# Norm factors by transposes, and a fixed order for the end of a two-layer transformer kernel

## The chip, the cores and the metric

The kernel runs on one core of a Trainium2 chip. The metric is device time in microseconds (us), the median over runs. TensorE (PE in the views; PEld is its weight load), VectorE (DVE), ScalarE (ACT) and GpSimd (POOL) each work through a list of instructions of their own and wait for one another by semaphores; SyncE (SP), ACT and POOL issue the transfers (DMA) between memory and the on-chip buffers. Products land in PSUM, which the kernel uses as eight banks of 128 x 512 fp32.

## What is computed

Two layers of a latent-diffusion backbone over 512 latent tokens and 256 context tokens, D = 1024, all in float32. Each layer is an attention mixer and a SwiGLU feed-forward, both behind a modulated RMS norm, and the result is the RMS-normed latent stream:

```python
def rms_norm(x, gain=None):
    y = x * lax.rsqrt(jnp.mean(x * x, axis=-1, keepdims=True) + EPS)
    return y if gain is None else y * gain
...
for l in range(DEPTH):                      # 2 layers, the second without context output
    a = modulate(h, shift, scale)           # rms_norm(h) * (1 + scale) + shift
    h = h + g_a * mixer(a)                  # layer 0: latent + neighbourhood heads; layer 1: sliding window
    h = h + g_f * swiglu(modulate(h, ...), w_gate_up, w_down)
return rms_norm(h_lat, final_norm)
```

Layer 0 also norms the two low-rank projections of its latent attention (256 and 128 features, with a gain).

## The kernel before, in words

Activations are stored transposed: eight tiles (`KT`), each 128 features by 768 tokens (`LATS`, 512 columns; `CTXS`, 256). Every large product is made of three: weights and activations are split into a high part and a rest (`h`, `lo`), and `mm3` (L328) and `product` (L1367) multiply high by high, high by rest and rest by high into one bank.

**A norm** needs one factor per token, and tokens lie along the free dimension. So every norm goes the same way. ACT squares the eight tiles (`square_sum`, L369) and POOL or DVE adds them up. PE multiplies each block of 128 tokens of the sum, as weights, by a column of ones, which leaves that block's sums in one column of PSUM, tokens along the partitions (L388, L802, L980). ACT takes the root (L390), DVE the reciprocal (L391): a narrow tile `col`, 128 x (2 to 4) values. To bring the factors back along the free dimension, in every partition, DVE builds a block-diagonal matrix, identity times `col` (L392, L806, L988), and PE multiplies it from the left by a 128 x 128 matrix of ones (L397, L812, L992). In `rstd` the factors are then read where they are, in the one bank with the tag `o`; in `norm_spread` and `gained` ACT copies them to a buffer `r` first (L814, L993).

There are twelve such norms. `first_norm` and `norm_spread` (L799 to L814) make the two at the start, latents and context, with a hand-written order on PE (`run`). `gained` (L963) makes two in the neighbourhood attention, with the gains of the low-rank projections, as side work between the steps of the attention. `rstd` (L379) makes eight: two each for the ends of the four `output` stages (both mixers' and both feed-forwards' last products). The stage `output` (L1242) runs two streams, each eight products of one output tile with the residual added by DVE (`add_residual`, L1223), and the squares behind it; the norm of the first stream is threaded between the second stream's products.

**The end of the kernel** is such a stage (`final1`, L1622): the last four of the 22 feed-forward columns, so 12 products of 128 x 256 for each output tile and half of the tokens (`HALVES`); eight tiles for the first half, then eight for the second with the weights kept. POOL adds the first six squares of a half to the running sum and DVE the last. `finished` (L1610) multiplies a tile by its norm's factors and its gain and sends it out, even tiles by SP, odd ones by ACT.

**The order.** A planner places the instructions at build time, by their priority (the order in which the program emits them, moved by hand for side work) and by its own simulated times, and gives out buffers and banks as they come free (`SCHED`). `behind(x, y)` and `in_turn` pin one instruction behind another without a wait on the data. Much around the `rstd` norms is pinned so: where a norm falls among later products, its sums and its spreading stand ahead of set products of those (L1262, L1458). Banks have tags: three `s`, two `t`, two `d`, one `o`; products take them in turn (`PG`), the side work only `d` (`PQ`), and in the neighbourhood attention so does every third set of transposes of the attention weights (`turned`, L497). Those, and `spread` (L365), which brings the softmax sums back, are PE transposes already.

## Time and profile before

| | |
|---|---|
| median of 3 runs | 1594.34 us (1590.8 to 1597.15) |
| the profiled execution | 1595.19 us, its span 1593.4 us, so 1.8 us lie around the span |
| PE | busy 96% of the span |
| DVE, ACT, POOL | 74%, 50%, 19% |
| mean granted clock of PE | 0.988 |
| last record of the last product | starts at 1580.33 us of the span |

Times in the views are us from the start of the span. In a row of the timeline the first number is the start, the second the duration; rows of like instructions that follow each other are merged (x4), and the brackets give the idle time of the engine before and what ended it. One fp32 product shows as two records. A PE record is longer than its turn: the next one starts while it still drains, so the cost on PE is read from start to start. The name behind an operation is out<-in, and for a product the moving operand comes first, then the weights.

### The profile page before, as it was taken

What the parts mean: (1) busy time and instruction counts of PE and PEld (TensorE: products, weight loads), DVE (VectorE), ACT (ScalarE), POOL (GpSimd) and SP (SyncE); (2) the same over time, 40 slices, a digit from 0 to 9 for tenths busy, and PEclk for the clock granted to TensorE, in tenths of its full rate; (3) what the DMA queues carried; (4) which work ended last, traced back from release to release, by engine and by line L of the source; (5) the groups of instructions that cost most, each with busy time, mean ns of one, the idle gap of its engine ahead of it and who ended that gap; (6) DMA issues with size and microseconds to landing.
All of it is one profiled execution on the core that took longest, in us unless ns stands there. A gap on an engine that the chain in (4) does not pass through costs nothing. (4 is left out here: it accounts for less than half of the span.)

```text
span 1593.4 us, 26482 instructions
## 1 busy us (share of the span) xinstructions
PE 1533.9 (96%) x9966; PEld 1371.9 (86%) x9966; DVE 1177.1 (74%) x2348; ACT 797.9 (50%) x1615; POOL 299.3 (19%) x322
## 2 busy tenths in 40 slices
PE   6999999999999999999999998999999999999997
PEld 4787767787899999999989896877889899899997
DVE  4885877576678587796858686878877778678685
ACT  4563676775455243342424243557755545354453
POOL 0144623320011101102021202493012000000002
PEclk9999999999999999999999998999999999999998
DMA  9745332104343555637464756121015133324222
GB/s 309 252 129 178 84 117 59 23 6 159 129 162 127 190 168 167 215 114 289 152 248 158 268 165 248 61 87 60 2 46 168 47 100 126 107 79 133 87 93 80
DMA packets 76544, 214.91 MB, mean 135 GB/s; under 512 B 9952, under 2 KB 17504, under 8 KB 76416
## 3 DMA queue, kind: packets, MB, share of 16 engines
q1 hardware_dynamic: 57568, 141.79, 27.0%
q0 software_dynamic: 15968, 67.24, 12.2%
q10 hardware_dynamic: 2880, 4.20, 0.7%
q8 instruction: 78, 1.28, 0.3%
q14 instruction: 50, 0.41, 0.1%
HBM read 186.97 MB, written 23.07 MB: 132 GB/s over the span
## 5 line engine op out<-in xcount | busy, mean ns | idle before, releaser
L324 ACT CAST wh<-wr 128x1024 fp32r<-128x1024 f32 (+2 forms) x148 | 114.7, 789 | 199.8 <-DMA wr<-in_w_dn_dram 35.4
L325 DVE TENSOR_TENSOR wl<-wr,wh 128x1024 fp32r<-128x1024 f32 (+2 forms) x145 | 134.0, 930 | 81.6 <-ACT wh L324 79.9
L555 ACT ACTIVATE p<-p,sm 128x512 f32<-128x512 f32 (+3 forms) x144 | 105.0, 730 | 30.2 <-DVE sm L559 28.3
L376 POOL TENSOR_TENSOR p<-p,p 128x256 f32<-128x256 f32 (+1 forms) x33 | 32.2, 976 | 465.0 <-PE psd L338 340.5
L1372 PE MATMUL pss<-b,wh 128*128 128x384 f32 (+1 forms) x344 | 107.0, 311 | 0.6 <-ACT b L361 0.6
L1373 PE MATMUL pss<-b,wh 128*128 128x384 f32 (+1 forms) x344 | 107.2, 312 | 0.1
L1374 PE MATMUL pss<-b,wl 128*128 128x384 f32 (+1 forms) x344 | 106.2, 312 | 0.4 <-DVE wl L1360 0.4
L233 DVE CUSTOM_DVE_ANT_0 p<-rope,cond 128x1024 bf16<-128x1024 f32 x64 | 77.2, 1222 | 38.3 <-DMA rope<-in_mod_w_dram 38.3
L337 PE MATMUL psd<-b,wh 128*128 128x512 f32 (+3 forms) x256 | 87.9, 344 | 0.0
L335 PE MATMUL psd<-b,wh 128*128 128x512 f32 (+3 forms) x216 | 78.5, 364 | 0.5 <-ACT wh L324 0.3
L549 PE MATMUL pso<-ph,b 128*64 128x256 f32 (+1 forms) x384 | 77.5, 360 | 0.4 <-DVE ph L494 0.2
L549 PE MATMUL pso<-pl,b 128*64 128x256 f32 (+1 forms) x384 | 76.7, 359 | 0.7 <-DVE pl L494 0.7
L338 PE MATMUL psd<-b,wl 128*128 128x512 f32 (+3 forms) x216 | 76.6, 355 | 0.1
L228 POOL DMA_DIRECT2D rope<-in_mod_w_dram x48 | 25.5, 531 | 239.7 <-DVE mod L233 227.0
L1374 PE MATMUL pst<-b,wl 128*128 128x384 f32 (+1 forms) x224 | 70.1, 313 | 0.0
L1373 PE MATMUL pst<-b,wh 128*128 128x384 f32 (+1 forms) x224 | 69.9, 312 | 0.0
L1372 PE MATMUL pst<-b,wh 128*128 128x384 f32 (+1 forms) x224 | 69.9, 312 | 0.0
L335 PE MATMUL pss<-st,wh 128*128 128x512 f32 (+2 forms) x200 | 68.2, 342 | 1.6 <-ACT st L1173 0.8
L338 PE MATMUL pss<-st,wl 128*128 128x512 f32 (+2 forms) x200 | 68.0, 341 | 0.0
L337 PE MATMUL pss<-b,wh 128*128 128x256 f32 (+3 forms) x211 | 67.9, 322 | 0.1
L749 PE MATMUL pss<-st,st 128*128 128x256 f32 (+3 forms) x194 | 60.3, 333 | 6.2 <-DVE sm L559 5.9
L1372 PEld LDWEIGHTS pss<-b,wh 128*128 128x128 f32 x344 | 65.2, 190 | 1.1 <-ACT b L361 0.9
(666 smaller groups left out, 5412.9 us busy)
## 6 DMA issues: line engine op xcount, KB each, us to landing
wr<-in_w_gu_dram SPq DMA_DIRECT2D x88, 512.0 KB, 4.1
rope<-in_mod_w_dram POOLq DMA_DIRECT2D x48, 512.0 KB, 3.8
wr<-in_w_out_dram SPq DMA_DIRECT2D x32, 512.0 KB, 3.5
wr<-in_w_dn_dram SPq DMA_DIRECT2D x64, 256.0 KB, 3.0
p<-home POOLq DMA_DIRECT2D x40, 384.0 KB, 5.4
home<-p POOLq DMA_DIRECT2D x40, 384.0 KB, 4.9
wr<-in_w_in_dram SPq DMA_DIRECT2D x21, 512.0 KB, 4.1
nb<-in_nb_dram SPq DMA_DIRECT2D x16, 384.0 KB, 3.1
```

What stands on the lines that cost most here:

```text
L233: V.tensor_tensor_reduce(out=T("p", [P, D], mybir.dt.bfloat16), in0=w, in1=cond[:, v, :], op0=ALU.mult, op1=ALU.add, scale=1.0, scalar=0.0 ...
L324: behind(S.copy(h, r), *after[:1])
L325: behind((G if eng else V).tensor_tensor(lo, r, f(h), op=ALU.subtract), *after[1:])
L335: ins = PE.matmul(o, wh[:, k], mh[:, c], start=first and k == 0, stop=False)
L337: PE.matmul(o, wh[:, k], ml[:, c], start=False, stop=False)
L338: PE.matmul(o, wl[:, k], mh[:, c], start=False, stop=last and k == n - 1)
L549: ins = PE.matmul(o[64 * i : 64 * i + 64, c], v(kt), t, start=n == 0, stop=n == len(moving[i]) - 1)
L555: S.activation(p[:, c], p[:, c], AF.Exp, bias=nm, scale=-1.0, accum_out=dn)
L749: PE.matmul(o, x, ks[0][:, keys], start=True, stop=False)
L1372: PE.matmul(o, wh, xh, start=first and k == 0, stop=False, skip_group_check=not first)
L1373: PE.matmul(o, wh, xl, start=False, stop=False, skip_group_check=not first)
L1374: PE.matmul(o, wl, xh, start=False, stop=k == 3, skip_group_check=not first)
```

## The change

Three things are done.

1. **Factors by transposes.** No diagonal matrix is built. For each block of 128 tokens, `spread` transposes the column of `col`, read as 128 equal columns (`to_broadcast`), which writes the factors of the block along the free dimension of all 128 partitions. This replaces L392 and L397 in `rstd`, L806 and L812 at the start, and L988 and L992 in `gained`. The mark `diag`, behind which a residual of the second stream is pinned, is now the reciprocal.
2. **No copy in `gained`.** The new `gain` lets DVE multiply the tiles by the factors where they are, in the bank of tag `d`, in two pieces (512 and 256 columns), where ACT copied them to `r` and DVE multiplied 768 columns at once.
3. **A fixed order at the end.** `final1` no longer uses `output` and `Norm`. The table of the root is loaded by a dummy root behind the last SiLU. The squares are kept as four partial sums per half (tiles 0 to 3 added by POOL, 4 and 5 by DVE, 6 and 7 alone), and PE adds them up: eight products of one column into one bank, in a chain, of which the first alone clears the bank (`start`). In the second half the products of tiles 0 to 7 are pinned in order, the sums of the first half in front of tile 2, its spreading in front of tile 3, and DVE's order is pinned throughout: two outputs of the first half in front of each of the residuals 5, 6 and 7, and two after. The first half's outputs all go out by SP, the second's by SP and ACT in turn.

```diff
@@ -381,20 +381,19 @@
 
         n, accs = c.stop - c.start, [x for x in acc if x is not None] if type(acc) is list else [acc]
         m, d = n // P, get()
-        col, diag = T("sm", [P, 6, 2]), B(tag=tag)
-        col = col.rearrange("p a b -> p (a b)")[:, :m]
+        col = T("sm", [P, 6, 2]).rearrange("p a b -> p (a b)")[:, :m]
         for i in range(m):
             for j, a in enumerate(accs):
                 marks["sum"] = PE.matmul(d[:, i : i + 1], a[:, i * P : (i + 1) * P], ones[:, :1], start=j == 0,
                                          stop=j == len(accs) - 1)
         marks["root"] = S.activation(col, d[:, :m], AF.Sqrt, bias=eps, scale=1.0 / nfeat)
-        V.reciprocal(col, col)
-        marks["diag"] = V.tensor_tensor(diag[:, :n].rearrange("p (a b) -> p a b", b=P), ident.unsqueeze(1).to_broadcast([P, m, P]),
-                                        col.unsqueeze(2).to_broadcast([P, m, P]), op=ALU.mult)
+        marks["diag"] = V.reciprocal(col, col)
         for i in range(0, n, 512):
             w = min(512, n - i)
             d = get() if r is not None else PS("o")
-            marks["spread"] = PE.matmul(d[:, :w], ones, diag[:, i : i + w], start=True, stop=True)
+            for j in range(0, w, P):
+                at = (i + j) // P
+                marks["spread"] = spread(d[:, j : j + P], col[:, at : at + 1].to_broadcast([P, P]))
             if r is None:
                 return d
             S.copy(r[:, c.start + i : c.start + i + w], d[:, :w])
@@ -798,19 +797,17 @@
 
     def first_norm(acc, c):
         n, d = (c.stop - c.start) // P, PM()
-        col, diag = T("sm", [P, 6, 2]).rearrange("p a b -> p (a b)")[:, :n], B(tag="p")
+        col = T("sm", [P, 6, 2]).rearrange("p a b -> p (a b)")[:, :n]
         ins = [PE.matmul(d[:, i : i + 1], acc[:, i * P : (i + 1) * P], ones[:, :1], start=True, stop=True) for i in range(n)]
         run(ins[0], ins[-1])
         root = S.activation(col, d[:, :n], AF.Sqrt, bias=eps, scale=1.0 / D)
         V.reciprocal(col, col)
-        V.tensor_tensor(diag[:, : n * P].rearrange("p (a b) -> p a b", b=P), ident.unsqueeze(1).to_broadcast([P, n, P]),
-                        col.unsqueeze(2).to_broadcast([P, n, P]), op=ALU.mult)
-        return root, diag
-
-    def norm_spread(diag, c):
+        return root, col
+
+    def norm_spread(col, c):
         d = PM()[:, : c.stop - c.start]
-        ins = PE.matmul(d, ones, diag[:, : c.stop - c.start], start=True, stop=True)
-        run(ins, ins)
+        ins = [spread(d[:, i * P : (i + 1) * P], col[:, i : i + 1].to_broadcast([P, P])) for i in range((c.stop - c.start) // P)]
+        run(ins[0], ins[-1])
         S.copy(r[:, c], d)
 
     fetched = []
@@ -960,6 +957,17 @@
 
         return use
 
+    def gain(tiles, g0, col):
+
+        for c in (LATS, CTXS):
+            d, n = PQ(), c.stop - c.start
+            for i in range(n // P):
+                at = c.start // P + i
+                spread(d[:, i * P : (i + 1) * P], col[:, at : at + 1].to_broadcast([P, P]))
+            for j, t in enumerate(tiles):
+                V.scalar_tensor_tensor(t[:, c], t[:, c], gains[:, g0 + j : g0 + j + 1], d[:, :n], op0=ALU.mult, op1=ALU.mult)
+        return tiles
+
     def gained(groups):
 
         d, m = PQ(), NT // P
@@ -984,17 +992,7 @@
         V.reciprocal(col, col)
         yield
         for i, (tiles, g0) in enumerate(groups):
-            diag, r = B(), B()
-            V.tensor_tensor(diag.rearrange("p (a b) -> p a b", b=P), ident.unsqueeze(1).to_broadcast([P, m, P]),
-                            col[:, i * m : i * m + m].unsqueeze(2).to_broadcast([P, m, P]), op=ALU.mult)
-            for c in (LATS, CTXS):
-                d = PQ()
-                PE.matmul(d[:, : c.stop - c.start], ones, diag[:, c], start=True, stop=True)
-                S.copy(r[:, c], d[:, : c.stop - c.start])
-            res = []
-            for j, t in enumerate(tiles):
-                V.scalar_tensor_tensor(t, t, gains[:, g0 + j : g0 + j + 1], r, op0=ALU.mult, op1=ALU.mult)
-                res.append(split(t, V))
+            res = [split(t, V) for t in gain(tiles, g0, col[:, i * m : i * m + m])]
             groups[i] = res
             yield
 
@@ -1424,7 +1422,7 @@
 
         def tail(self):
             product(self.z, self.s4, self.ops["22"])
-            S.activation(self.s[:, self.c2], self.z, AF.Silu)
+            marks["silu"] = S.activation(self.s[:, self.c2], self.z, AF.Silu)
             product(self.y, self.u2, self.ops["T4"])
             V.tensor_tensor(self.t[:, self.c1], self.y, self.t[:, self.c1], op=ALU.add)
             for c in (self.c2, self.c1) if self.w > NX else (slice(0, 2 * self.w),):
@@ -1607,11 +1605,6 @@
     output(lambda m: I["w_out1"][m], O, 1, 2, ((HALVES[1], 0), (HALVES[0], 0)), norm, (0, 0), wait=1)
 
 
-    def finished(m, r, c, v):
-        o = B(tag="p")
-        V.scalar_tensor_tensor(o[:, c], H[m][:, c], fn[:, m : m + 1], r[:, c], op0=ALU.mult, op1=ALU.mult)
-        (nc.sync, nc.scalar)[m % 2 if OUTQ else 0].dma_start(out[m, :, c], o[:, c])
-
     fn = const("final_norm", [P, 8])
 
     def down1(m, w, hs):
@@ -1620,8 +1613,68 @@
         add_residual(m, o, 1, 5, 0, LATS)
 
     def final1(src, hs):
-        keep = lambda src, m: ahead.get(m) or load_w(src(m), len(hs), P, None, "b")
-        output(src, hs, 1, 5, STREAMS1, Norm(H, finished, G if EF else None), (0, 0), None, keep, wait=1)
+
+        behind(S.activation(T("part", [P, 1]), eps, AF.Sqrt), marks["silu"])
+        kept, first = [], []
+
+        def root(sq, d):
+            ins = []
+            for a in sq:
+                for i in range(2):
+                    x = PE.matmul(d[:, i : i + 1], a[:, i * P : (i + 1) * P], ones[:, :1], start=not ins,
+                                  stop=a is sq[-1], skip_group_check=True)
+                    ins = [behind(x, *ins)]
+            col = T("sm", [P, 6, 2]).rearrange("p a b -> p (a b)")[:, :2]
+            S.activation(col, d[:, :2], AF.Sqrt, bias=eps, scale=1.0 / D)
+            return ins[0], col, V.reciprocal(col, col)
+
+        def factors(col):
+            d = PS("o")[:, :NX]
+            return d, [spread(d[:, i * P : (i + 1) * P], col[:, i : i + 1].to_broadcast([P, P])) for i in range(2)][-1]
+
+        def outputs(d, c, ms, queues):
+            res = []
+            for m in ms:
+                o = B(tag="p")
+                res.append(V.scalar_tensor_tensor(o[:, c], H[m][:, c], fn[:, m : m + 1], d, op0=ALU.mult, op1=ALU.mult))
+                queues[m % len(queues)].dma_start(out[m, :, c], o[:, c])
+            return res
+
+        def square(m, c, sq):
+            t = B(tag="p")[:, :NX]
+            S.activation(t, H[m][:, c], AF.Square)
+            if m in (0, 4, 6, 7):
+                sq.append(t)
+                return []
+            return [(G if m < 4 else V).tensor_tensor(sq[-1], sq[-1], t, op=ALU.add)][m < 4 :]
+
+        for c in HALVES:
+            sq, turn = [], []
+            for m in range(KT):
+                if c is HALVES[0]:
+                    kept.append(ahead.get(m) or load_w(src(m), len(hs), P, None, "b"))
+                elif m == 2:
+                    last, col, ins = root(first, PQ())
+                    turn.append(ins)
+                elif m == 3:
+                    d, last = factors(col)
+                elif m > 4:
+                    turn += outputs(d, HALVES[0], (2 * m - 10, 2 * m - 9), (nc.sync,))
+                o = PG()[:, :NX]
+                ins = mm3([(o, c)], kept[m], hs)
+                if c is HALVES[1]:
+                    behind(ins, last)
+                last = ins
+                turn.append(add_residual(m, o, 1, 5, 0, c))
+                turn += square(m, c, sq)
+            if c is HALVES[0]:
+                first = sq
+            else:
+                turn += outputs(d, HALVES[0], (6, 7), (nc.sync,))
+            in_turn(*turn)
+        _, col, ins = root(sq, PQ())
+        d, _ = factors(col)
+        in_turn(turn[-1], ins, *outputs(d, c, range(KT), (nc.sync, S)))
 
     ffn(1, ops, sums, HALVES, ("st",) * 4, norm.marks[0], lambda j: 0, down1, final1)
```

## The prediction

> **What bounds the kernel now.** The first view is the page's head, the second the table of stretches (busy us of each engine, then the granted clock as a share of full speed, the share of the DMA engines, GB/s).
>
> ```profile
> span 1593.4 us, 26482 instructions
> PE 1533.9 (96%) x9966; PEld 1371.9 (86%) x9966; DVE 1177.1 (74%) x2348; ACT 797.9 (50%) x1615; POOL 299.3 (19%) x322
> ```
>
> ```profile
> 0.00:20.00 20.00, 7.38 (x42) 3.48 (x42) 5.94 (x11) 8.66 (x15) 2.08 (x8) 1.00 0.93 336
> 20.00:60.00 40.00, 36.99 (x243) 27.64 (x240) 26.69 (x66) 20.47 (x44) 0.00 (x0) 0.96 0.94 328
> ...
> 200.00:430.00 230.00, 218.80 (x1514) 178.79 (x1514) 158.66 (x387) 150.15 (x332) 47.91 (x36) 0.97 0.24 79
> 430.00:480.00 50.00, 50.00 (x300) 48.63 (x299) 35.69 (x64) 29.84 (x55) 6.47 (x12) 1.00 0.48 166
> ...
> 900.00:1200.00 300.00, 286.62 (x1877) 246.96 (x1877) 230.46 (x547) 168.32 (x348) 92.77 (x82) 0.98 0.32 112
> ...
> 1557.00:1593.00 36.00, 25.84 (x202) 24.77 (x201) 20.20 (x46) 11.36 (x25) 8.91 (x12) 0.87 0.24 79
> ```
>
> PE bounds nearly everything. It is busy for all of 430 to 480, where two of the changed norms lie, and for 95% of the attention stretches. So a norm inside the kernel is worth the time that it takes of PE's own list, not the latency of its chain, because later products cover the chain. Only two places have PE idle for long: the first 20 us, and the end, 10.2 of the last 36 us. At the end the chain itself counts. The timeline there, PE, DVE and ACT in turn:
>
> ```profile
> 1580.33 0.28 PE L338 MATMUL pss<-st,b 128*128 128x256 f32 x1
> 1583.89 1.01 PE L388 MATMUL psd<-ones,p 128*128 128x1 f32 x4 [3.28 <-DVE p L376]
> 1585.91 1.22 PE L397 MATMUL pso<-p,ones 128*128 128x256 f32 x2 [1.01 <-DVE p L392]
> ```
>
> ```profile
> 1569.73 0.48 DVE L1223 SCALAR_TENSOR_TENSOR b<-pst,mod,b 128x256 f32<-128x256 f32 x1 [0.96 <-PE pst L338]
> 1571.17 0.48 DVE L1223 SCALAR_TENSOR_TENSOR b<-pss,mod,b 128x256 f32<-128x256 f32 x1 [0.96 <-PE pss L338]
> ...
> 1581.04 0.48 DVE L1223 SCALAR_TENSOR_TENSOR b<-pss,mod,b 128x256 f32<-128x256 f32 x1
> 1581.80 1.70 DVE L1612 SCALAR_TENSOR_TENSOR p<-b,final_norm,pso 128x256 f32<-128x256 f32 x4 [0.29 <-DMA out_dram<-p]
> 1583.42 0.42 DVE L376 TENSOR_TENSOR p<-p,p 128x256 f32<-128x256 f32 x1
> 1585.23 0.17 DVE L391 RECIPROCAL sm<-sm 128x2 f32<-128x2 f32 x1 [1.40 <-ACT sm L390]
> 1585.43 0.42 DVE L392 TENSOR_TENSOR p<-ident_r,sm 128x256 f32<-128x256 f32 x1
> 1587.17 3.22 DVE L1612 SCALAR_TENSOR_TENSOR p<-b,final_norm,pso 128x256 f32<-128x256 f32 x8 [1.31 <-PE pso L397]
> ```
>
> ```profile
> 1558.93 0.62 ACT L324 CAST b<-wr 128x512 fp32r<-128x512 f32 x1 [1.14 <-PE psd L1373]
> ...
> 1572.18 1.28 ACT L390 ACT_TABLE_LOAD   x1
> ...
> 1581.61 0.42 ACT L373 ACTIVATE p<-b 128x256 f32<-128x256 f32 x1 [0.43 <-DVE b L1223]
> 1584.94 0.26 ACT L390 ACTIVATE sm<-psd,eps 128x2 f32<-128x2 f32 x1 [2.92 <-PE psd L388]
> ```
>
> The last product drains at T = 1580.33 + 0.28 = 1580.61. Its residual starts 0.43 late, since DVE was giving out the first half's results. The square is done at 1582.03, but the add (L376) starts only at 1583.42, behind four more outputs (L1612). Then come sums, root, reciprocal, diagonal and spreading one after the other, and eight outputs that end at 1587.17 + 3.22 = 1590.39, T + 9.8. The remaining 3.0 us to the span's end are the last transfer, which stays.
>
> **The price of the parts.** The kernel holds transposes of this shape already; the first row below gives the records' min/median/max in ns, the second six in a run. The next two, of the chain, are the spreading and the sums of a norm at full speed, for 256 tokens.
>
> ```profile
> L367 PE MATMUL pst<-ident_r,pl x80: 270/273/328, 220.3 to 1174.1; 128*128 128x128 f32 x80
> ```
>
> ```profile
> 220.35 0.82 PE L367 MATMUL pst<-ident_r,pl 128*128 128x128 f32 x6
> ```
>
> ```profile
> 1578.99 0.45 PE pso L397 x2
> ```
>
> ```profile
> 1575.09 0.34 PE psd L388 x4
> ```
>
> Six transposes take 0.82 us, of which the last one drains 0.27, so they start (0.82 - 0.27) / 5 = 0.11 us apart. A product by ones costs 0.45 us for two blocks of 128 tokens, 0.225 each: a transpose saves 0.115 us a block. I take 0.11, the row's own spacing; that these weights are one column read 128 times over, the trace does not show, and the upper end is the full record, 0.27 a block, as if nothing overlapped.
>
> [...]
>
> **The norms ahead of the end**, on PE:
>
> ```profile
> 16.28 2.08 PE L812 MATMUL pst<-p,ones 128*128 128x512 f32 x2
> ```
>
> ```profile
> 204.48 1.56 PE L992 MATMUL psd<-b,ones 128*128 128x512 f32 x4
> 205.69 0.58 PE L749 MATMUL pss<-st,st 128*128 128x512 f32 x1
> ...
> 212.44 2.90 PE L992 MATMUL psd<-b,ones 128*128 128x512 f32 x4 [1.20 <-DVE b L988]
> 214.78 0.72 PE L749 MATMUL pss<-b,b 128*128 128x192 f32 x1
> ```
>
> - The start, four blocks: L812 takes 2.0 us, 2.2 times the 0.9 of full speed, so four transposes at that pace take 4 x 0.11 x 2.2 = 1.0, a saving of **1.0**. What follows is one PE list up to the first products, and PE is busy 37 of the next 40 us, so I count it whole; the DMA engines, 94% busy there, could take it back (lower end 0). The diagonal was hidden behind other products.
> - Context norm at the start: two blocks, **0.23**.
> - `gained`, first group: 1.21 us from start to start, six transposes 0.66: **0.55**.
> - Second group: PE waits 1.20 us for the diagonal and then needs 2.34 at half clock. The transposes need only `col`, ready long before (first row below), so the wait has no cause left, and six of them at half clock take 1.3. That is 1.0 + 1.2 = 2.2 us. But the attention there waits for its own softmax as well (last row: us in total, times, longest), so some of it will be handed on. I take half, **1.1**; ends 0 and 2.9 (no wait, full clock).
>
> ```profile
> 202.42 0.23 DVE L984 RECIPROCAL sm<-sm 128x12 f32<-128x12 f32 x1 [1.84 <-ACT sm L983]
> ```
>
> ```profile
> L988 DVE TENSOR_TENSOR b<-ident_r,sm x2: 950/954/957, 202.7 to 211.3; 128x768 f32<-128x768 f32 x2
> ```
>
> ```profile
> L993 ACT COPY b<-psd x4: 372/484/588, 207.1 to 215.4; 128x512 f32<-128x512 f32 x2, 128x256 f32<-128x256 f32 x2
> ```
>
> ```profile
> L996 DVE SCALAR_TENSOR_TENSOR b<-b,mla_gain,b x3: 1012/1019/1019, 208.0 to 216.7; 128x768 f32<-128x768 f32 x3
> ```
>
> ```profile
> 212.00:214.00 2.00, 1.55 (x2) 0.84 (x3) 0.64 (x3) 1.28 (x5) 1.65 (x1) 0.50 0.29 112
> ...
> 216.00:218.00 2.00, 2.00 (x9) 1.37 (x8) 2.00 (x4) 0.48 (x2) 0.00 (x0) 0.50 0.33 113
> ```
>
> ```profile
> PE pss L749 <- DVE sm L559: 4.3, 5, 1.8
> ```
>
> - In `gained` ACT loses four copies (1.9 us) and DVE two diagonals (1.9), while each of the three multiplications falls into two pieces, about 0.75 (an estimate between 0.48 for 256 and 1.02 for 768 columns) and 0.48, together 0.6 more. Both engines gain, off the path: nothing counted. The price is that a bank of tag `d` stays occupied for up to two multiplications, 1.5 us, instead of one copy of 0.59. Attention transposes queue on PE for that bank, and the products behind them too: 0 to 2 us over both groups, taken as 0, for the freed DVE starts the multiplications earlier.
> - Six `rstd` norms, with 384 + 384, 512 + 256 and 256 + 256 tokens: 16 blocks at 0.115, **1.85**.
>
> Together 1.0 + 0.23 + 0.55 + 1.1 + 1.85 = **4.7 us** less. At 0.27 for a transpose, 34 blocks cost 34 x 0.16 = 5.4 us more than that, and the sum is 0.7 us lost.
>
> **The end.** In front of the last product, PE gets the first half's sums as eight products instead of two: 16 records instead of 4, 12 x 0.34 / 4 = 1.0 more, and 0.23 less for the spreading: **0.8 us lost**, for PE is gapless there. The table load moves from an idle place (1572.18) to another (ACT idles 1.14 in front of 1558.93): nothing; without that cover 1.28 on the cast of the last weights.
>
> Behind it DVE is pinned. Products end 1.44 us apart (1571.17 - 1569.73). Residual 4 is done at T - 3.8, outputs 0 and 1 (0.40 each, 3.22 / 8) at T - 3.0, residual 5 at T - 2.4. The add of tile 5 must wait for its square (0.09 + 0.42), done at T - 1.45; it holds up all that is queued behind it: outputs 2 and 3 until T - 0.65, residual 6 until T - 0.2, outputs 4 and 5 until T + 0.6, residual 7 until T + 1.1 (before: T + 0.9). The square ends at T + 1.6. Now PE adds at once. The other six products of the chain are done in the meantime, two remain: 0.34 at full clock, 1.01 at the 0.50 of the row below; I take 0.7. Root and reciprocal with their hand-overs take 0.5, two transposes 0.11 + 0.27 = 0.4 to 0.9, taken as 0.5, eight outputs 3.2. That is T + 6.7, **3.1 us** sooner (3.4 warm, 2.5 cold); the wait behind four outputs and the diagonal are what goes.
>
> ```profile
> 1584.00:1585.00 1.00, 0.90 (x4) 0.81 (x4) 0.00 (x0) 0.06 (x1) 0.00 (x0) 0.50 0.82 269
> ```
>
> **Sum**: 4.7 - 0.8 + 3.1 = 7.0 us off the profiled 1595.19 (span 1593.4 and 1.8 around it), 1588.2. That execution lies 0.85 over the median, so the median goes from 1594.34 to **1587.3 us**.
>
> **Rivals.**
> 1. *The clock does the rest.* From 212 to 218 PE runs at half clock behind two idle spells, and so do sums and spreading at the end. If the spell without the diagonal stays too short for the clock to fall, 6 us at half speed become 3; with the wait gone whole (1.8 more) and a warm end (0.3), the gain is 12, to 1582. For it: PE's pause at the end shrinks from 3.3 to under 1 us. Against it: the softmax wait of 1.8 us at 208 stays. [...] Chance 0.23.
> 2. *Transposes don't overlap.* Each takes its 0.27: norms +0.7, end -2.3, so 1.6 us off: 1592.7. For it speaks only the record; against it the run of six. [...] Chance 0.12.
> 3. *The end doesn't shorten*, so that this part does not do what it says: DVE's pinned row, already late by my own working, waits for an output buffer as before (0.29) or the add once more. If residual 7 slips by 3.1 us more, the gain is 3.9: 1590.4. Chance 0.1.
> 4. *Slower: the planner's new order in the attention.* Everything not pinned is placed anew, and bank `d` frees later. PE idles 11.2 us in 200 to 430 and 13.4 in 900 to 1200. If that grows by half, 12.3 us, the result is 5.3 slower, 1599.6; it decides from 7 us, 28% more idle. For it: such waits are many and small. Against it: DVE and ACT have less to do there. Chance 0.12.
>
> **How the numbers follow.** My forecast, 1585 to 1590, has 0.43. About 0.5%, 8 us, is what a measurement of this kernel can tell from no change. Faster by that: most of rival 1 and a third of the forecast, 0.37. Slower by that: under half of rival 4, 0.05. The rest, 0.58, lies within. The range, 1580.5 to 1595, takes in rivals 1 to 3 and leaves out most of rival 4 and the far end of rival 1.
>
> **What would show it.** Right: rows of the new transposes 0.11 apart; no wait for L988 near 212, and less time at half clock; PE full from 430 to 480 with 0.35 us less in each norm; 16 sum records ahead of the second half's tile 2; from the last product to the last output 6.7 us. Wrong: transposes 0.27 apart; new PE waits for tag `d` in 195 to 225; idle time of 200 to 430 or 900 to 1200 changed by more than 5 us, which would be the planner and none of my terms; residual 7 more than 1.5 us behind the last product.

## The result, and the profile after

| | before | after |
|---|---|---|
| median, first comparison (7 runs each) | 1594.34 us | 1585.67 us (1583.14 to 1590.18) |
| ratio, 95% interval | | 0.9945, 0.9927 to 0.9962 |
| the same two kernels again (35 and 12 runs) | 1593.05 us | 1590.35 us |
| ratio, 95% interval | | 0.9976, 0.9955 to 0.9996 |
| profiled execution, span | 1595.19, 1593.4 us | 1590.18, 1588.4 us |

The changed kernel is faster, by 0.2 to 0.6%. The forecast (7.0 us off, 0.44%) lies between the two comparisons. The profiled execution of the changed kernel is the slowest of its seven, although none of them has a higher granted clock (0.995), so the two spans show less than the medians do.

The same stretches as before, and the last 36 us (columns: the engines' busy us, granted clock, DMA share, GB/s):

```profile
0.00:20.00 20.00, 7.48 (x49) 4.60 (x49) 5.25 (x10) 9.41 (x17) 2.08 (x8) 1.00 0.94 335
20.00:60.00 40.00, 37.74 (x237) 28.07 (x238) 26.57 (x66) 20.06 (x43) 0.00 (x0) 1.00 0.95 331
200.00:430.00 230.00, 220.14 (x1565) 182.57 (x1566) 160.92 (x396) 152.28 (x334) 48.31 (x37) 0.99 0.27 84
430.00:480.00 50.00, 50.00 (x303) 49.09 (x302) 36.73 (x65) 30.67 (x57) 5.91 (x11) 1.00 0.48 161
900.00:1200.00 300.00, 285.13 (x1896) 247.79 (x1895) 228.19 (x545) 168.56 (x348) 93.69 (x81) 0.99 0.33 112
1552.00:1588.00 36.00, 29.15 (x244) 28.76 (x243) 20.25 (x46) 12.18 (x27) 4.60 (x6) 0.94 0.29 89
```

In 200 to 430 PE idles 9.9 us instead of 11.2, and the clock is 0.99 instead of 0.97, which over 230 us is some 4.6 us of full clock. At the end PE idles 6.9 us of 36 instead of 10.2. From 430 to 480 nothing can be read off, since PE is full in both; there only the distance between two landmarks tells. The end, PE and then DVE:

```profile
1578.62 0.28 PE L338 MATMUL pst<-st,b 128*128 128x256 f32 x1
1578.74 1.39 PE L1624 MATMUL psd<-ones,p 128*128 128x1 f32 x12
1580.44 0.61 PE L1624 MATMUL psd<-ones,p 128*128 128x1 f32 x4 [0.31 <-ACT p L1645]
1581.70 0.40 PE L367 MATMUL pso<-ident_r,sm 128*128 128x128 f32 x2 [0.65 <-DVE sm L1629]
```

```profile
1577.16 0.42 DVE L1649 TENSOR_TENSOR p<-p,p 128x256 f32<-128x256 f32 x1 [0.61 <-ACT p L1645]
1577.51 0.86 DVE L1639 SCALAR_TENSOR_TENSOR p<-b,final_norm,pso 128x256 f32<-128x256 f32 x2
1578.29 0.48 DVE L1221 SCALAR_TENSOR_TENSOR b<-pss,mod,b 128x256 f32<-128x256 f32 x1
1578.68 0.86 DVE L1639 SCALAR_TENSOR_TENSOR p<-b,final_norm,pso 128x256 f32<-128x256 f32 x2
1579.46 0.48 DVE L1221 SCALAR_TENSOR_TENSOR b<-pst,mod,b 128x256 f32<-128x256 f32 x1
1579.86 0.86 DVE L1639 SCALAR_TENSOR_TENSOR p<-b,final_norm,pso 128x256 f32<-128x256 f32 x2
1581.38 0.17 DVE L1629 RECIPROCAL sm<-sm 128x2 f32<-128x2 f32 x1 [0.66 <-ACT sm L1628]
1582.14 3.22 DVE L1639 SCALAR_TENSOR_TENSOR p<-b,final_norm,pso 128x256 f32<-128x256 f32 x8 [0.59 <-PE pso L367]
```

T is 1578.90 here. The last residual begins at T + 0.56, behind two outputs; twelve records of the last sums are already done on PE when the last square comes, four remain, and the last output ends at 1585.36, T + 6.5 (before T + 9.8). Measured from the start of the last product's last record, which is how all kernels below are compared, this "tail" is 6.74 us instead of 10.06.

In the neighbourhood attention, PE's two sets of transposes and PE's waits from 200 to 260 (us in total, times, longest):

```profile
205.78 0.87 PE L367 MATMUL psd<-ident_r,sm 128*128 128x128 f32 x6
208.10 0.82 PE L367 MATMUL psd<-ident_r,sm 128*128 128x128 f32 x6
...
212.84 0.63 PE L502 MATMUL psd<-ident_r,p 128*128 128x128 f32 x4 [1.54 <-DVE b L968]
```

```profile
PE psd L758 <- DVE b L493: 2.6, 1, 2.6
PE psd L502 <- DVE b L968: 1.5, 1, 1.5
PE pss L748 <- DVE sm L558: 0.8, 1, 0.8
```

Both sets run at full clock (granted 1.00 from 200 to 212) and wait for nothing. A new wait of 1.5 us has come: the transposes of the attention weights (L502) want the bank of tag `d` that DVE's multiplications (L968) still read. What it cost in all only the experiments can say.

### The profile page after: what moved, and what is told of

The parts are those of the page before. It is cut to its first block, busy times and chain, and to the rows that moved or that the text cites. A ratio compares the mean times of both kernels' runs of the same rounds, so it can differ in the third digit from the quotient of the medians.

```text
span 1588.4 us, 26532 instructions
## 1 busy us (share of the span) xinstructions
PE 1527.7 (96%) x10000; PEld 1370.7 (86%) x10000; DVE 1167.0 (73%) x2339; ACT 796.4 (50%) x1612; POOL 294.2 (19%) x316
## 5 line engine op out<-in xcount | busy, mean ns | idle before, releaser
L337 PE MATMUL psd<-b,wh 128*128 128x512 f32 (+3 forms) x256 | 87.4, 342 | 0.0
L1649 POOL TENSOR_TENSOR p<-p,p 128x256 f32<-128x256 f32 x6 | 4.6, 766 | 348.4 <-ACT p L1645 348.2
L1372 PEld LDWEIGHTS pss<-b,wl 128*128 128x128 f32 x344 | 65.0, 190 | 2.9 <-DVE wl L1358 2.8
```

Source lines behind the costliest of these rows:

```text
L337: PE.matmul(o, wh[:, k], ml[:, c], start=False, stop=False)
L1372: PE.matmul(o, wl, xh, start=False, stop=k == 3, skip_group_check=not first)
```

## The experiments

To find where the time goes, each profile is cut at landmarks that all kernels share: from the sums of the start's first norm to those of its second ("start"); from the first score of the neighbourhood attention to that of the latent attention ("attention"); from the second sums of the norm of w_out0 to the first sums of feed-forward 0's norm ("feed-forward 0"); and the tail. Old means that a kernel keeps before's code there. All in us; each number is one execution.

| kernel | ratio to before, 95% interval | start | attention | feed-forward 0 | tail |
|---|---|---|---|---|---|
| before | 1 | 37.7 | 87.4 | 524.1 | 10.06 |
| after | 0.9945 (0.9927 to 0.9962) | 37.7 | 81.4 | 525.4 | 6.74 |
| e1 after again | 0.9976 (0.9955 to 0.9996) | 37.2 | 81.2 | 526.2 | 6.99 |
| e2 new end alone | 0.9985 (0.9966 to 1.0005) | 36.6 old | 84.5 old | 521.6 old | 6.74 |
| e3 new `gained` alone | 0.9970 (0.9953 to 0.9986) | 37.6 old | 78.6 | 522.9 old | 9.67 old |
| e7 diagonals early | 0.9993 (0.9975 to 1.0011) | 38.0 old | 82.0 | 521.3 old | 10.08 old |
| e4 new norms alone | 0.9981 (0.9966 to 0.9996) | 37.4 | 84.9 old | 524.5 | 7.89 |
| e6 transposes twice | 0.9947 (0.9929 to 0.9965) | 36.5 | 80.4 | 526.3 | 6.74 |
| e5 factors copied | 0.9932 (0.9913 to 0.9950) | 36.8 | 79.1 | 523.9 | 6.99 |
| e8 two sums at the end | 0.9938 (0.9914 to 0.9962) | 38.1 | 80.1 | 525.8 | 6.26 |
| e10 old `rstd` | 0.9988 (0.9971 to 1.0006) | 36.3 | 78.4 | 523.5 old | 6.73 |
| e11 e5 and e8 | 0.9934 (0.9915 to 0.9953) | 36.6 | 80.4 | 526.8 | 6.26 |
| e12 e11, old `rstd` | 0.9970 (0.9954 to 0.9986) | 35.7 | 77.7 | 524.6 old | 6.26 |
| e9 diagonal at the end | 0.9968 (0.9953 to 0.9984) | 38.1 | 80.0 | 525.9 | 7.86 |

Before ran in three later comparisons with medians of 1593.05 (beside e1, e2, e3, e7), 1594.92 (e4, e6, e5, e8) and 1593.27 us (e10, e11, e12, e9). e1, e2, e3 and e7 ran on one chip, the other experiments on another; for the first comparison no chip is on record. The five ratios below 0.995 rest on 6 or 7 runs of the kernel each, all others on 12. And e6, which only adds work to the changed kernel, has 0.9947 beside the 0.9976 of e1. So totals that differ by 0.3% between comparisons are not put down to the code below; the rows and the landmarks carry the argument.

**e1, the changed kernel once more**, without an edit.

> The changed kernel once more. In its first profile it lost 2 us again between the last norm of the second mixer (1224.80, 3.8 earlier than before) and the last product (1578.62, 1.7 earlier), and 1.1 between 460 and 986. If that is part of the change (the planner's new order), this profile has the same idle time of PE there: 4.7 us in 700 to 900, 2.4 in 1240 to 1480. If it is the scatter of one execution, those stretches come nearer to before (1.3 and 2.1), and the span falls to about 1584.

1590.35 us. The tail, the attention and feed-forward 0 come out as in the first profile, to 0.8 us, and PE idles 5.2 us from 700 to 900 (4.7 in the first profile, 1.3 in before): what is lost there belongs to the changed kernel and not to one execution of it. The total lies 4.7 us higher than in the first comparison. The granted clock is lower too (0.9907 on average against 0.9929), which goes with some of that (last section).

**e2, the new end alone.** Before, with the mark for the table load and the new `final1`, transposes included:

```diff
-        output(src, hs, 1, 5, STREAMS1, Norm(H, finished, G if EF else None), (0, 0), None, keep, wait=1)
+        behind(S.activation(T("part", [P, 1]), eps, AF.Sqrt), marks["silu"])
...
+        in_turn(turn[-1], ins, *outputs(d, c, range(KT), (nc.sync, S)))
```

> The kernel before with the new end alone. Theory (each part acts in its own place): from the start of the last product's last record to the last output 6.7 us as in the changed kernel, 10.1 before; 0.8 lost in front of it; 2.3 to 2.5 us in all, ratio 0.9985; 200 to 430 as before, with PE at half clock around 212. Rival (the gain is the planner's new order): a shorter end, but some of the 5.6 us that were gained between 207 and 234 as well.

1592.09 us, 2.4 us less than before by the ratio, with an interval that still holds no change; the tail is 6.74. In the attention, where its code is before's, PE runs at half clock around 212 as it does there (granted 0.50 from 212 to 216 in both).

**e3, the new `gained` alone.**

```diff
-            diag, r = B(), B()
...
+            res = [split(t, V) for t in gain(tiles, g0, col[:, i * m : i * m + m])]
```

> The kernel before with the transposes in the two norms of the neighbourhood attention alone. Theory: the whole 5.6 us between 207 and 234 come from here, no half clock there, a wait of 1.5 us for the bank; the first norm of the first mixer's end at 428.4 instead of 434.0, ratio 0.9965. Rival (the planner's order from the start on does it): less than 2 us gained there.

1589.11 us: 4.8 us less (2.2 to 7.5), by its middle the largest single part of the change, though the intervals of e2 and e4 overlap with it. The attention takes 78.6 us instead of 87.4, 84.5 and 84.9 with the old code.

**e7, the diagonals early.** Before, with both diagonals built right behind the reciprocal; the products by ones and the copies stay:

```diff
-        yield
-        for i, (tiles, g0) in enumerate(groups):
-            diag, r = B(), B()
+        diags = [B() for _ in groups]
+        for i, diag in enumerate(diags):
...
+        yield
+        for i, (tiles, g0) in enumerate(groups):
+            diag, r = diags[i], B()
```

> The kernel before, but both diagonals of the two norms in the neighbourhood attention are built right behind the reciprocal, ahead of the first group's work. The products by ones stay. Theory (the gain there is the wait for the diagonal and the half clock that follows, not the cheaper transposes): the wait of 1.2 us goes and with it the half clock, 3 to 5 of the 5.6 us come. Rival (the transposes themselves): at most 1.2 us for the wait, the products still run at half clock.

82.0 us in the attention, 3.6 under the mean of the old code (85.6) and 2.5 under the shortest of the three; seven kernels with the new `gained` take 80.0 on average, 5.6 less than the old code. PE's wait for the diagonal is gone. So that wait and what it brings are about half of the 5.6 us or more, as far as one execution can say. The total, 0.9993 (1.1 us less, with an interval from 4.0 less to 1.8 more), does not resolve it.

**e4, the new `rstd` and `first_norm` alone**; the end keeps its old order, but its factors come by transposes:

```diff
             d = get() if r is not None else PS("o")
-            marks["spread"] = PE.matmul(d[:, :w], ones, diag[:, i : i + w], start=True, stop=True)
+            for j in range(0, w, P):
+                at = (i + j) // P
+                marks["spread"] = spread(d[:, j : j + P], col[:, at : at + 1].to_broadcast([P, P]))
```

> The kernel before with the transposes in the start's two norms and the eight norms of the output stages alone; in the end they stand in the old order. Theory: at the start 1.0 us is won until 18 us and gone by 50 (PE stays at half clock that much longer), each later norm wins 0.23 to 0.46 of PE's list, 1.6 us for six, and the end wins the diagonal and some of the product, about 1.3: 2.9 us in all, ratio 0.998. 200 to 430 as before. Rival (the saving at the start is kept): 1.0 more, to be seen at 50 us.

1591.58 us, 3.0 us less, of which the tail has 2.0. That is not all the transposes' own: the last square's add ends 2.9 us behind the start of the last product's last record instead of 3.5 in before, and the last sums take 0.61 us instead of the 1.01 of before, where the granted clock was 0.50.

**e6, every transpose of `rstd` and of the start twice.**

```diff
-                marks["spread"] = spread(d[:, j : j + P], col[:, at : at + 1].to_broadcast([P, P]))
+                for _ in range(2):
+                    marks["spread"] = spread(d[:, j : j + P], col[:, at : at + 1].to_broadcast([P, P]))
```

> The changed kernel with every transpose of a factor made twice, in the start's two norms and in the six norms ahead of the end, 22 transposes more. By the spacing of 0.11 in a run each later norm takes 0.22 to 0.44 more of PE's list (1.76 in all), ratio to the changed kernel 1.001; by the full record of 0.27, 4.3. At the start four more at half clock are 1.0 us: if the clock rises at a set time they are gone by 50 us, if PE's list decides they are still there.

From the first to the second sums of w_out0's norm PE is full, and that distance prices the spreading of three blocks: 32.03 us in each of before, e2, e3 and e7, 31.74 in after, e1, e4, e5 and e8, 32.05 here (and again 32.03 with the old `rstd` of e10 and e12). Three more transposes cost 0.31 us, 0.10 each. The first row is the changed kernel's spreading there, the second all its transposes into the bank of tag `o`, with min, median and max ns:

```profile
432.91 0.49 PE L367 MATMUL pso<-ident_r,sm 128*128 128x128 f32 x3
```

```profile
L367 PE MATMUL pso<-ident_r,sm x22: 270/272/295, 53.4 to 1581.8; 128*128 128x128 f32 x22
```

Three take 0.49 us of which 0.27 is the last one's record, so they start 0.11 apart. The record's 0.27 is not what a transpose costs. At the start the doubled ones take 1.97 us, nearly what the products by ones took (2.08), and yet the start is not longer (36.5 us):

```profile
16.24 1.97 PE L367 MATMUL pst<-ident_r,sm 128*128 128x128 f32 x8
```

**e5, the factors copied.** In `gain`, ACT copies the factors to `r` again, and DVE multiplies 768 columns:

```diff
+        r = B()
...
-            for j, t in enumerate(tiles):
-                V.scalar_tensor_tensor(t[:, c], t[:, c], gains[:, g0 + j : g0 + j + 1], d[:, :n], op0=ALU.mult, op1=ALU.mult)
+            S.copy(r[:, c], d[:, :n])
+        for j, t in enumerate(tiles):
+            V.scalar_tensor_tensor(t, t, gains[:, g0 + j : g0 + j + 1], r, op0=ALU.mult, op1=ALU.mult)
```

> The changed kernel, but in the two norms of the neighbourhood attention ACT copies the factors to a buffer, and DVE multiplies 768 columns at once, as before. Theory (the wait of 1.5 us of the attention's transposes behind the multiplications is the bank being held): this wait goes, but the copies come back on ACT, 1.9 us; between the same and 1.5 us faster. Rival (DVE is late there anyway, or the copy is what frees DVE): the wait stays or the multiplications come later, up to 2 us slower.

1583.12 us. The wait for the bank is gone; PE's longest waits from 200 to 260 in this kernel are these:

```profile
PE pss L748 <- DVE sm L558: 2.5, 3, 1.3
PE pst L502 <- DVE pl L493: 0.6, 1, 0.6
```

But the softmax waits, 0.8 us in the changed kernel, are 2.5 now. The three kernels with the copy take 79.1, 80.4 and 77.7 us in the attention, 79.1 on average against 80.0 without: by these rows the bank's wait is mostly handed on. The total lies 2.6 us under the changed kernel's first median and 7.2 under its second. That is more than the attention shows, and where it comes from is open.

**e8, two partial sums for the first half**, and its outputs 4 to 7 behind the last residual:

```diff
-            if m in (0, 4, 6, 7):
+            if m in ((0, 4) if c is HALVES[0] else (0, 4, 6, 7)):
...
-                elif m > 4:
+                elif m in (5, 6):
...
-                turn += outputs(d, HALVES[0], (6, 7), (nc.sync,))
+                turn += outputs(d, HALVES[0], (4, 5, 6, 7), (nc.sync,))
```

> The changed kernel with two partial sums instead of four in the first half (tiles 0 to 3 and 4 to 7), and with only two outputs of the first half ahead of each of the residuals 6 and 7's predecessors (0 and 1 ahead of 5, 2 and 3 ahead of 6), four behind residual 7. Theory: 8 sum records fewer on a gapless PE, 0.7 us; residual 7 starts at once, not 0.6 late, so 6.1 to 6.3 us from the last product's last record to the last output instead of 6.7. 1.2 us in all, ratio to the changed kernel 0.9993, too little for the times, to be read in the rows. Rival (the end waits for output buffers or for the reciprocal behind four outputs): nothing won behind the last product.

The tail is 6.26 us, 0.5 less: the two outputs in front of residual 7 had held it up, as the prediction's own working said. The 0.7 us that eight sum records fewer were to save ahead of the last product did not come. PE now waits for DVE's add between them, and from the first of these sums to the next product it is 1.53 us instead of 1.70:

```profile
1567.61 0.60 PE L1624 MATMUL psd<-ones,p 128*128 128x1 f32 x4 [0.57 <-DVE p L1649]
```

The total, 1584.97, cannot show half a microsecond.

**e9, the diagonal at the end.** The changed kernel, where both halves of the end build the diagonal and multiply it by ones:

```diff
-            return ins[0], col, V.reciprocal(col, col)
+            V.reciprocal(col, col)
+            diag = B(tag="p")[:, :NX]
...
-            return d, [spread(d[:, i * P : (i + 1) * P], col[:, i : i + 1].to_broadcast([P, P])) for i in range(2)][-1]
+            return d, PE.matmul(d, ones, diag, start=True, stop=True)
```

> The changed kernel, with the diagonal and one product by ones instead of two transposes in both halves of the kernel's end; order and partial sums stay. With the transposes alone the stretch behind the last product fell by 2.0 us (7.89 against 9.67 to 10.08), with the whole new end by 3.2 (6.74 to 6.99). If the two parts add up, the order alone gives 1.2 to 1.5 and this kernel ends 8.3 to 8.8 us behind its last product. If the diagonal and its product cost only what their rows say (0.42 and two hand-overs of 0.06, and 0.45 to 1.2 for the product instead of 0.4), it ends 7.4 to 8.0 us behind. In the rest of the kernel no difference: about 1 us slower than the changed kernel.

```profile
1579.11 0.17 DVE L1629 RECIPROCAL sm<-sm 128x2 f32<-128x2 f32 x1 [0.66 <-ACT sm L1628]
1579.31 0.42 DVE L1631 TENSOR_TENSOR p<-ident_r,sm 128x256 f32<-128x256 f32 x1
1581.05 1.26 DVE L1642 SCALAR_TENSOR_TENSOR p<-b,final_norm,pso 128x256 f32<-128x256 f32 x3 [1.32 <-PE pso L1636]
```

From the reciprocal to the first output it is 1.94 us here and in before, 0.76 in after (1581.38 to 1582.14) and in e4. Not all of these 1.2 us are the transposes' own: the product by ones ran at a granted clock of 0.50 here (1.22 us), after's transposes at 1.00 (0.40 us). In e1 and e5 the transposes took 0.66 us, and there it is 1.01. So of the 3.3 us of the tail the transposes have 0.9 where they too are slow (7.86 against 6.99), and the order has 1.8 (e3's 9.67 against 7.86; in both the last sums take 0.6 us and the product by ones 1.22). The other 0.6 are the slower rows of single executions: 0.4 in before's last sums (1.01 us, granted 0.50) and 0.25 in the transposes. The forecast by rows (7.4 to 8.0) held; the one that took e4's 2.0 for the transposes' share did not.

**e10, the old `rstd`** in the changed kernel, **e11, the copy of e5 with the sums of e8**, and **e12, e11 with the old `rstd`**:

```diff
-        marks["diag"] = V.reciprocal(col, col)
+        V.reciprocal(col, col)
+        marks["diag"] = V.tensor_tensor(diag[:, :n].rearrange("p (a b) -> p a b", b=P), ident.unsqueeze(1).to_broadcast([P, m, P]),
+                                        col.unsqueeze(2).to_broadcast([P, m, P]), op=ALU.mult)
```

> The changed kernel with the old `rstd` (diagonal and products by ones) in the six norms that use it; the norms of the start, `gained` and the kernel's end stay changed. Theory A, that the new `rstd` loses more in feed-forward 0, where the planner lays out everything anew, than it saves in its norms: from the second sum of w_out0's norm to the first sum of feed-forward 0's norm 522.5 us (old `rstd` in four executions: 521.3 to 524.1) instead of 525.3 (new: 523.9 to 526.3), PE idle under 3 us in 700 to 900, and w_out0's and w_out1's norms back at 32.03 and 21.72; net about 2 us faster than the changed kernel, about 1584. Theory B, that those 2.8 us come from elsewhere in the change: the stretch stays at 525, the norms cost 0.3 and 0.2 more each, and the kernel is about 1 us slower than the changed one. Behind the last product 6.7 to 7.0 us by both.

> The changed kernel with both variants that did well alone: ScalarE copies the factors out of the bank in `gain` and VectorE multiplies 768 columns at once, and the first half's eight squares at the end go into two partial sums, with its outputs 0 and 1 ahead of residual 5, 2 and 3 ahead of 6, and 4 to 7 behind residual 7. If the two add up: about 79 to 80 us from the first score of the neighbourhood attention to that of the latent attention, 6.3 us behind the last product, and 2.5 us less than the changed kernel in all, about 1583. If the gain of the copy was only the lottery of the half clock around 212 us: 80 to 81 there, and about 1585.

> As the kernel with the copy in `gain` and two partial sums at the end, but with the old `rstd`. By theory A of the kernel with the old `rstd` alone it is another 2 us faster, about 1581, with 522.5 us from the second sum of w_out0's norm to feed-forward 0's norm; by theory B it is 0.5 to 1 us slower than with the new `rstd`.

1590.61, 1582.82 and 1589.01 us. The profiles alone would have misled: those of e10 and e12 show the shortest spans of the four (1580.4 and 1583.1 us), but they are the fastest of the twelve executions of their kernels, and e11's is the slowest of its seven. By the medians the old `rstd` costs 6.2 us in e12 against e11, and in e10 4.9 or 0.3 against the changed kernel's two medians. So theory A, by which the new `rstd` loses more than it saves, has nothing for it, and theory B's 0.5 to 1 us may be too small. But no landmark holds 6 us (e12's attention and feed-forward 0 are shorter than e11's), so the size stays open. Feed-forward 0 with the old `rstd` took 523.5 and 524.6 us, between the 522.5 of the four kernels with few changes and the 525.6 of the eight with the new one, so neither theory has the cause of the 3 us there. e11 has the lowest median of all, 1582.82, but its ratio does not part from that of e5 (0.9932), of e8 (0.9938) or of after's first comparison.

## Why the prediction was right, and where it was not

The sign and the range held; 1585 to 1590 took in the first median, and the second, 1590.35, lies 0.4 above it. Taken by stages, with averages over the kernels that share the code, the gain is about 5.6 us: 5.6 less in the attention, 0.5 in the norms of w_out0 and w_out1, 3.1 in the tail, 0.3 at the start, against 0.8 more ahead of the last product and 3.1 more in feed-forward 0. That the sum came out near 7.0 is luck in part: the attention gave about 4 us more than its terms, and feed-forward 0 took 3.1 that no term held.

- **Price of a transpose: right.** 0.11 from start to start forecast, 0.10 to 0.11 measured. Rival 2 is out.
- **`rstd`: right on PE, as far as it could be priced.** 0.115 a block forecast; 0.29 for three blocks of w_out0 (32.03 to 31.74) and 0.22 for two of w_out1 (21.72 to 21.50) measured, 0.10 and 0.11.
- **The start: failed.** The step was "so I count it whole". The transposes do take 1.12 us instead of 2.08, and the next products come earlier:

```profile
16.18 1.12 PE L367 MATMUL pst<-ident_r,sm 128*128 128x128 f32 x4
...
22.04 0.79 PE L758 MATMUL pss<-wh,b 128*128 128x512 f32 x1 [1.08 <-ACT b L422]
...
24.30 0.63 PE L759 MATMUL pss<-wh,b 128*128 128x512 f32 x1
24.73 0.63 PE L760 MATMUL pss<-wh,b 128*128 128x512 f32 x1
...
27.65 1.07 PE L828 MATMUL pst<-st,cond_col 128*32 128x256 f32 x16
```

  In before the first large product starts at 22.66, 0.62 later; but there the products fall from 0.43 apart to 0.23 at 26.96, and here they are 0.43 apart to the last one. L828 comes at 27.65 instead of 27.75. In 14 profiles the change of pace comes anywhere from 24.3 us to beyond 27, and in e6, with twice the transposes, at 25.2, so it does not follow the work in front of it. Work removed ahead of it is then worth what it would cost at full pace, for these four blocks 4 x 0.115 = 0.5 us (an estimate from the prediction's rows), and not the 1.0 of the slow pace. The start took 37.1 us on average in nine kernels with single transposes (35.7 to 38.1), 37.5 in four without; these 0.3 us, in that scatter, fit the 0.5 or nothing better than the 1.0.
- **`gained`: right in its mechanism, undersized.** Forecast 0.55 + 1.1; measured 4.8 (2.2 to 7.5) by e3's ratio and 5.6 by the landmarks. The step that failed is "I take half", for the second group: the wait for the diagonal and the products behind it went whole, and by the landmarks more than its upper end of 2.9 came. From 212 to 216, before and then after:

```profile
212.00:216.00 4.00, 3.56 (x9) 2.38 (x10) 0.85 (x4) 2.23 (x7) 2.35 (x1) 0.50 0.19 65
```

```profile
212.00:216.00 4.00, 3.16 (x20) 2.01 (x20) 4.00 (x12) 3.27 (x8) 3.44 (x2) 1.00 0.24 81
```

  PE does 20 records there instead of 9. The clock's share in this is chance in part: the clock of that window is 0.50 to 0.82 in the three kernels with the old code, and with the new one 1.00 in after and e3, 0.77 in e1 and 0.50 in e6. And it is not the larger share. e2, with the old code, and e6, with the new, both run at 0.50 from 210 to 216, and at the same mean clock from 200 to 260, e2 and then e6:

```profile
200.00:260.00 60.00, 53.55 (x372) 42.35 (x370) 47.06 (x101) 43.85 (x102) 18.76 (x15) 0.94 0.31 94
```

```profile
200.00:260.00 60.00, 56.52 (x409) 44.89 (x408) 46.05 (x110) 46.09 (x109) 23.08 (x20) 0.94 0.32 96
```

  PE idles 3.5 us instead of 6.4, and the attention takes 80.4 us instead of 84.5. The wait for the diagonal (0.8 us in e2) is gone, two more waits for DVE fall from 2.6 and 1.7 us to 0.3 and 0.4, and the bank's 1.5 us is new. What freed DVE for those two was not tried alone.
- **The price of bank `d`, taken as 0 of 0 to 2:** a wait of 1.5 us did come, one of the prediction's own signs of being wrong. Without it (e5, e11, e12) the attention is 0.9 us shorter on average, less than kernels of the same code differ.
- **The end: right.** T + 6.7 forecast, T + 6.5 measured (T + 6.7 in e1 and e5), with the late residual, the square's wait ahead of the add and the outputs where the working had them. The table load found its cover: the view lists no wait of PE from 1540 to the last product. Rival 3 is out. The term for the sums in front of the last product was too small: from their first record to the next product it is 1.70 us instead of 0.36, and for the spreading 0.14 instead of 0.25, so 1.2 us are lost where 0.8 was forecast. The distance from the norm of w_out1 to the last product, 353.2 us on average with the new end and four sums (352.8 to 353.8) against 352.4 with the old order (351.7 to 353.2), shows 0.8, within that scatter.
- **Rival 1, the clock: in part.** The changed kernel's medians stay above 1582. The transposes at the end took 0.40 us in after, at a granted clock of 1.00, and 0.66 in e1 and e5, where PE paused no longer than 0.65 us between the last product and the transposes; so the warm end came in some executions only. Which pause is short enough no run shows: behind 3.29 us the last sums took 0.61 us in e3 and 1.01 in e7.
- **Not seen: feed-forward 0.** The planner lays it out anew, and PE idles more from 700 to 800, before and then after:

```profile
700.00:800.00 100.00, 100.00 (x577) 95.82 (x576) 76.47 (x134) 34.68 (x64) 15.46 (x29) 1.00 0.56 194
```

```profile
700.00:800.00 100.00, 97.44 (x557) 92.35 (x557) 71.45 (x124) 33.36 (x62) 14.93 (x28) 1.00 0.55 190
```

  PE's two longest waits there in the changed kernel are for DVE's subtractions that make the rests of weights (`wl`); in before the view lists no wait of PE:

```profile
PE pst L1372 <- DVE wl L1358: 1.2, 1, 1.2
PE pss L1372 <- DVE wl L1358: 1.1, 1, 1.1
```

  DVE itself waits for a load of weights in this stretch, 2.62 us where before has 0.99:

```profile
749.09 0.69 DVE L1392 TENSOR_TENSOR pl<-wr 128x512 f32<-128x512 f32 x1 [2.62 <-DMA wr<-in_w_gu_dram]
```

  Rival 4 had the mechanism, but looked for it in the attention. Which edit moves the planner so is left open: with the old `rstd` half of it stays, and in e6, whose feed-forward 0 is as long, those two waits are not there and others are.

The parts do not add up in the totals: 2.4 (e2), 4.8 (e3) and 3.0 us (e4) make 10.2, of which e2 and e4 both count the 1.2 us of the last norm's transposes, and the whole gave 8.7 and 3.8. The intervals, some 2.5 us to either side each, are wide enough for that.

## What to carry to other kernels

Bring per-token factors back along the free dimension by transposes of the broadcast column rather than by a diagonal and a product: it takes one instruction and one hand-over out of the chain, and what that is worth is decided by where the chain is exposed (0.9 us at the kernel's end, 7.86 against 6.99), not by the PE time saved (0.1 us a block). Count work that is removed from a slow start at what it costs at full pace, and not at the slow one (here the start took 37.1 us instead of 37.5, where 1.0 was counted). And where single executions differ by more than the change is worth, compare stages between landmarks over several kernels that share the code, and take the total from many runs: one profile can be the fastest or the slowest of its kernel.

## What the runs showed of the hardware

The scatter of this kernel goes with the clock that PE is granted. Over 81 later executions of before the times run from 1587.01 to 1602.72 us and the mean granted clock from 0.985 to 0.994, with a correlation of -0.75 and 1.4 us for each 0.001. The fastest quarter has 1589.7 us at a clock of 0.9909, the slowest 1598.4 at 0.9872. The half-clock spells (windows of 4 us with a granted clock of 0.50 to 0.89) stand in the same few places in all kernels (20 to 28, 180, 208 to 220, 245, 950 to 988, 1062 to 1070 and the end; e6 has one at 814), but not all of them in each execution. The executions of before have a mean clock of 0.9889, those of the changed kernel 0.9929 (first comparison) and 0.9907 (second), those of e5 and e11 0.9935 and 0.9937. At 1.4 us for 0.001, 2.5 to 5.6 us of the changed kernel's lead go with the clock. That is a correlation and no cause, and it fails at times: the slowest of the changed kernel's first seven executions, 1590.18 us, has 0.995, and none of them has more. The granted clock does not show all either: in after it reads 1.00 from 20 to 60, while its first large products start 0.43 us apart there and those of before, at the same length, 0.23 from 26.96 on. What decides whether a spell comes in an execution was not tried.
